# Sparse attention on one Trainium2 core: local keys ahead of selected keys

## The chip, the cores and the metric

The program runs on one core of one Trainium2 chip. The metric is the device time of one execution in microseconds (us); the time before is the median of three runs. One execution was also recorded by the hardware profiler; all rows below are from that one.

A core has five engines that run side by side, each with its own in-order queue: TensorE (PE in the rows; its weight loads are a row of their own, PEld), VectorE (DVE), ScalarE (ACT), GpSimd (POOL) and SyncE (SP), which here issues transfers. They wait for each other by semaphores.

## What is computed

One decoder layer on 512 tokens of width 1024. The part that the change touches is the sparse attention (NSA): 8 query heads in two groups of four (`kv`), each query attending three times, to compressed keys (31 blocks), to selected key blocks and to a local window of 256 keys, with a linear distance bias. The three results are summed with gates:

```
s = einsum(q, k_cmp) - slope * dist;  p_cmp = masked_softmax(s);  o_cmp = p_cmp @ v_cmp
s = einsum(q, kg)    - slope * dist;  p_slc = masked_softmax(s);  o_slc = p_slc @ vg
s = einsum(q, kwb)   - slope * dist;  p_win = masked_softmax(s);  o_win = p_win @ vwb
return gb[..., 0:1] * o_cmp + gb[..., 1:2] * o_slc + gb[..., 2:3] * o_win
```

With 512 tokens all 8 key blocks are selected, so the selected keys are simply all earlier keys. Around this part stand the input projections, gated linear attention (GLA), cross-attention to a memory and a gated convolutional feed-forward layer.

## The kernel before

Matmuls keep fp32 accuracy by splitting each operand into a high and a low part; `split` (lines 164 to 166) makes the high part on ScalarE and the low part, source minus high, on VectorE. A dense product takes three matmuls per tile (lines 160 to 162).

The attention runs over eight blocks, `kv` 0 and 1 with `i` 0 to 3 each; block `i` holds 128 queries. The main loop (lines 695 to 701) writes, for each block, first `nsa_values` of the block before, then `nsa_scores` of this one, then some "fillers": dense products of the GLA stage, two, one, two, one, one, two, none and none of them, which give TensorE work while the softmax runs.

`nsa_scores` makes, for each of four heads `g`, the scores of the selected keys (n = 128(i+1) columns) and of the local keys (nw, up to 384 columns), each added to its bias and reduced to a row maximum in one VectorE instruction (lines 603 and 615). Then come the compressed scores on GpSimd and ScalarE with their row sums (line 627), and eight exponentials on ScalarE (line 631), selected and local in turn, each followed by a read of its row sum. Only then one reciprocal and one product with the gates (lines 634 and 635) make the 12 coefficients `cf` per query. All probabilities are scaled by them: selected keys on VectorE for g 0 to 2 (line 639) and on ScalarE for g 3 (641), local keys on ScalarE for g 0 and 2 (643) and on GpSimd for g 1 and 3 (645), compressed keys on GpSimd (646).

`nsa_values` takes the scaled probabilities key tile by key tile: four transposes into a bank `pt` (line 669, two such banks), a split of that bank, and the products with the values (line 663) into one bank `o`. The order of these jobs is selected, local, compressed; the last, compressed one needs one product, the others two. Two small additions and splits make the block's output.

The order of the instructions on an engine is not the order of this text: the framework's scheduler, when the kernel is built, places an instruction whose operands it expects to be ready ahead of earlier ones that are not. In the trace, filler matmuls (lines 160 to 162, and 197 to 199 of GLA) stand between transposes and products. Once built, the order is fixed.

Of the kernel before, what the change touches and what calls it, by code (L numbers as in the profile page):

```python
# [9 lines left out]
F32 = mybir.dt.float32  # L10
# [6 lines left out]
P = 128  # L17
# [41 lines left out]
def layer_kernel(ctx: ExitStack, tc: tile.TileContext, xT, memT, W, small, const, gfin, out, out_t, order):  # L59
# [19 lines left out]
    def s_(dtype=F32):  # L79
        return sb([P, T], dtype, "s", SB)  # L80
# [6 lines left out]
    def bank(tag):  # L87
        uid[0] += 1
        return psum.tile([P, T], F32, name=f"{stage[0]}_ps_{tag}_{uid[0]}", tag=tag, bufs=BANKS[tag])
# [14 lines left out]
    def C(name):  # L104
        a, b = CO[name]
        return cst[:, a:b]
# [460 lines left out]
    def nsa_scores(kv, i):  # L567
        n = P * (i + 1)
        j0 = max(0, i - 2)
        nw = P * (i + 1 - j0)  # L570
        off = (2 - (i - j0)) * P
        qs = slice(i * P, (i + 1) * P)
        mx = sb([P, 12], F32, "mx", 3)
        sums = sb([P, 12], F32, "sums", 3)
        cm = CM[i % 2][:, :, 0:31]

        def compressed():
            ps = bank("sc")
            pv = ps[:, 0:248].rearrange("p (g n) -> p g n", n=62)
            for g in range(4):  # L580
                nc.tensor.matmul(pv[:, g, :], Q2[kv * 4 + g][:, qs], KC[:, kv, :], start=True, stop=True)
            bias = C("cmp")[:, i * 31:(i + 1) * 31].unsqueeze(1).to_broadcast([P, 4, 31])
            nc.vector.tensor_tensor(cm, pv[:, :, 0:31], bias, op=ALU.add)
            nc.vector.tensor_tensor(cm, pv[:, :, 31:62], cm, op=ALU.add)
            nc.vector.tensor_reduce(mx[:, 0:4], cm, axis=AX.X, op=ALU.max)

        first = kv == 0 and i == 0
        if not first:
            compressed()
        ss, sw = [], []  # L590
        for g in range(4):
            q = Q2[kv * 4 + g][:, qs]
            ps = bank("sc")
            if i < 2:

                both = ps[:, 0:2 * n].rearrange("p (b n) -> p b n", b=2)
                nc.tensor.matmul(both, q, KX[kv][0][:, :, :n], start=True, stop=False)
                nc.tensor.matmul(both, q, KX[kv][1][:, :, :n], start=False, stop=True)
            else:
                nc.tensor.matmul(ps[:, :n], q, KS[kv][0][:, :n], start=True, stop=False)  # L600
                nc.tensor.matmul(ps[:, :n], q, KS[kv][1][:, :n], start=False, stop=True)
            s = s_()
            nc.vector.tensor_tensor_reduce(out=s[:, :n], in0=ps[:, :n], in1=C("slc")[:, 384 - P * i:512],
                                           op0=ALU.add, op1=ALU.max, scale=1.0, scalar=-3e38,
                                           accum_out=mx[:, 4 + g:5 + g])
            ss.append(s)
            if i < 2:
                ps = ps[:, n:2 * n]
            else:
                ps = bank("sc")  # L610
                ks = slice(j0 * P, j0 * P + nw)
                nc.tensor.matmul(ps[:, :nw], q, KW[kv][0][:, ks], start=True, stop=False)
                nc.tensor.matmul(ps[:, :nw], q, KW[kv][1][:, ks], start=False, stop=True)
            s = s_()
            nc.vector.tensor_tensor_reduce(out=s[:, :nw], in0=ps[:, :nw], in1=C("win")[:, off:off + nw],
                                           op0=ALU.add, op1=ALU.max, scale=1.0, scalar=-3e38,
                                           accum_out=mx[:, 8 + g:9 + g])
            sw.append(s)
        if first:
            compressed()  # L620
        nm = sb([P, 12], F32, "nm", 3)
        nc.vector.tensor_mul(nm, mx, C("nslope")[:, kv * 12:(kv + 1) * 12])  # L622
        nc.gpsimd.tensor_tensor(cm, cm, C("slope")[:, kv * 4:kv * 4 + 4].unsqueeze(2).to_broadcast([P, 4, 31]),
                                op=ALU.mult)
        nc.gpsimd.tensor_tensor(cm, cm, nm[:, 0:4].unsqueeze(2).to_broadcast([P, 4, 31]), op=ALU.add)
        nc.scalar.activation(cm, cm, AF.Exp)
        nc.vector.tensor_reduce(sums[:, 0:4], cm, axis=AX.X, op=ALU.add)
        for g in range(4):
            sl = 2.0 ** -(kv * 4 + g + 1)
            for s, c, w in ((ss[g], 4 + g, n), (sw[g], 8 + g, nw)):  # L630
                nc.scalar.activation(s[:, :w], s[:, :w], AF.Exp, scale=sl, bias=nm[:, c:c + 1],  # L631
                                     accum_out=sums[:, c:c + 1])
        cf = sb([P, 3, 4], F32, "cf", 3)
        nc.vector.reciprocal(cf.rearrange("p b g -> p (b g)"), sums)
        nc.vector.tensor_mul(cf, cf, gates[i][:, kv * 12:(kv + 1) * 12].rearrange("p (g b) -> p b g", b=3))
        for g in range(4):
            a, b = ss[g][:, :n], sw[g][:, :nw]
            if g < 3:
                nc.vector.tensor_scalar(a, a, cf[:, 1, g:g + 1], None, op0=ALU.mult)
            else:  # L640
                nc.scalar.activation(a, a, AF.Copy, scale=cf[:, 1, g:g + 1])
            if g % 2 == 0:
                nc.scalar.activation(b, b, AF.Copy, scale=cf[:, 2, g:g + 1])
            else:
                nc.gpsimd.tensor_scalar(b, b, cf[:, 2, g:g + 1], None, op0=ALU.mult)
        nc.gpsimd.tensor_tensor(cm, cm, cf[:, 0, :].unsqueeze(2).to_broadcast([P, 4, 31]), op=ALU.mult)
        return kv, i, j0, ss, sw, CM[i % 2]

    def nsa_values(kv, i, j0, ss, sw, cm):
# [1 line left out]
            for a in range(2):  # L651
                ON[kv * 2 + a] = (g_(F32R), g_(F32R))
        qs = slice(i * P, (i + 1) * P)
        jobs = [([ss[g][:, kt * P:(kt + 1) * P] for g in range(4)], V2[kt][:, kv, :]) for kt in range(i + 1)]
        for kt in range(j0, i + 1):
            jobs.append(([sw[g][:, (kt - j0) * P:(kt - j0 + 1) * P] for g in range(4)], V2[kt][:, 2 + kv, :]))
        jobs.append(([cm[:, g] for g in range(4)], VC[:, kv, :]))
        po = bank("o")
        last = len(jobs) - 1

# [5 lines left out]
        for j, (srcs, v) in enumerate(jobs):  # L666
            pt = bank("pt")
            for g in range(4):
                nc.tensor.transpose(pt[:, g * P:(g + 1) * P], srcs[g], C("ident"))  # L669
            if j < last:  # L670
                h, l = sb([P, T], F32R, "pth", 2), sb([P, T], F32R, "ptl", 2)
                split(h, l, pt)
                parts = (h, l)
            else:
                x = PC[i % 2]
                split(x[0:32], x[32:64], pt[0:32])
                parts = (x,)
            if ready is not None:
                product(*ready)
            ready = (j, v) + parts  # L680
# [635 lines left out]
```

## Time and profile before

| | before |
|---|---|
| median of 3 runs | 865.82 us (863.78 to 866.4) |
| the profiled execution | 864.57 us |
| its span, first to last instruction | 862.7 us |
| TensorE's granted clock, mean | 0.998 of full speed |
| the sparse-attention stage in the span | about 72 to 212 us |

The busy times of the page are shares of the span. In a view of stretches each engine has busy time and, in brackets, instructions started. A waits view names the engine and line that waited, what released it, total time, number of waits and the longest one. A wait of PEld is the weight load's; the matmul before it can still be running.

### The profile page before, as it was taken

The page shows a single profiled execution, that of the slowest core. Times are in us where ns is not written, and L with a number is a line of the kernel's source. Part 1 is how long each engine was busy: PE and PEld are TensorE (multiplying, and loading weights), DVE is VectorE, ACT ScalarE, POOL GpSimd, SP SyncE. Part 2 cuts the span into 40 slices and gives each one's busy share as a digit, 9 for nine tenths or more (in the row PEclk, how much of TensorE's full clock was granted, in tenths as well). Part 3 has the DMA queues.
Part 4 walks back from the last instruction along what each step waited for, and adds up shares of the span by engine and source line. Part 5 has one row for each costly group of instructions (what it writes and reads, how often), then busy time and mean ns, then how long its engine had stood idle before and what let it go on. Part 6 is the DMA issues. An engine that isn't in the chain of part 4 may idle for free.

```text
span 862.7 us, 11076 instructions
## 1 busy us (share of the span) xinstructions
PE 847.2 (98%) x4172; PEld 706.4 (82%) x4172; DVE 565.8 (66%) x923; ACT 425.0 (49%) x742; POOL 176.6 (20%) x157
## 2 busy tenths in 40 slices
PE   9999999999999999999999999999999999999997
PEld 6988788777877888898888888888888888888996
DVE  7576898989979677454587759665533465565324
ACT  8466878787444455344455545433311333334311
POOL 2373354412000023203200412111000111112121
PEclk9999999999999999999999999999999999999999
DMA  8332210102221242254331132222222222222302
GB/s 292 115 131 98 74 50 25 49 25 74 74 91 57 74 147 98 97 178 147 123 115 49 65 110 96 98 98 97 98 98 98 97 98 98 97 98 98 123 25 98
DMA packets 26406, 83.58 MB, mean 97 GB/s; under 512 B 3056, under 2 KB 5104, under 8 KB 26352
## 3 DMA queue, kind: packets, MB, share of 16 engines
q1 hardware_dynamic: 26064, 82.58, 27.5%
q8 instruction: 33, 0.54, 0.2%
q10 hardware_dynamic: 288, 0.28, 0.1%
q14 instruction: 21, 0.17, 0.1%
HBM read 80.76 MB, written 2.10 MB: 96 GB/s over the span
## 4 chain that ended last, share of the span: by engine, by line
PE 87%; DVE 5%; ACT 4%; issue 1%; POOL 1%; DMA 0%; DVEq 0%; ACTq 0%; POOLq 0%
PE up_ps_sc L162 4%; PE up_ps_sc L161 4%; PE up_ps_sc L160 4%; PE fill_ps_acc L160 3%; PE fill_ps_acc L161 3%; PE fill_ps_acc L162 3%; PE up_ps_pt L162 3%; PE up_ps_pt L161 3%; PE up_ps_pt L160 3%; PE up_ps_acc L162 3%; PE up_ps_acc L161 3%; PE up_ps_acc L160 3%; PE nsa_ps_o L663 2%; PE nsa_ps_pt L669 2%; PE down_ps_sc L162 2%; PE down_ps_sc L161 2%
## 5 line engine op out<-in xcount | busy, mean ns | idle before, releaser
L1086 POOL TENSOR_TENSOR up_s<-up_s,up_s 128x512 f32<-128x512 f32 x22 | 35.8, 1630 | 259.1 <-ACT up_wh L140 207.0
L141 DVE TENSOR_TENSOR up_wl<-up_raw,up_wh 128x1024 fp32r<-128x1024 f32 x40 | 63.0, 1575 | 15.4 <-ACT up_wh L140 15.3
L140 ACT ACTIVATE up_wh<-up_raw 128x1024 fp32r<-128x1024 f32 x40 | 42.5, 1061 | 60.9 <-PE up_ps_sc L161 31.9
L160 PE MATMUL up_ps_sc<-xo_g,up_wh 128*128 128x512 f32 x124 | 48.3, 390 | 0.0
L162 PE MATMUL up_ps_sc<-xo_g,up_wl 128*128 128x512 f32 x124 | 48.3, 389 | 0.0
L161 PE MATMUL up_ps_sc<-xo_g,up_wh 128*128 128x512 f32 x124 | 48.3, 389 | 0.0
L160 PE MATMUL up_ps_pt<-xo_g,up_wh 128*128 128x512 f32 x104 | 40.5, 389 | 0.0
L162 PE MATMUL up_ps_pt<-xo_g,up_wl 128*128 128x512 f32 x104 | 40.5, 389 | 0.0
L161 PE MATMUL up_ps_pt<-xo_g,up_wh 128*128 128x512 f32 x104 | 40.5, 389 | 0.0
L160 PE MATMUL fill_ps_acc<-in_g,fill_wh 128*128 128x512 f32 x96 | 38.4, 400 | 0.8 <-DVE fill_t L548 0.8
L161 PE MATMUL fill_ps_acc<-in_g,fill_wh 128*128 128x512 f32 x96 | 38.1, 397 | 0.0
L162 PE MATMUL fill_ps_acc<-in_g,fill_wl 128*128 128x512 f32 x96 | 37.9, 395 | 0.0
L631 ACT ACTIVATE nsa_s<-nsa_s,nsa_nm 128x128 f32<-128x128 f32 (+3 forms) x64 | 34.2, 538 | 6.5 <-DVE nsa_nm L622 6.5
L160 PE MATMUL up_ps_acc<-xo_g,up_wh 128*128 128x512 f32 x88 | 34.3, 389 | 0.0
L162 PE MATMUL up_ps_acc<-xo_g,up_wl 128*128 128x512 f32 x88 | 34.3, 389 | 0.0
L161 PE MATMUL up_ps_acc<-xo_g,up_wh 128*128 128x512 f32 x88 | 34.2, 389 | 0.0
L1082 ACT ACTIVATE up_s<-up_s 128x512 f32<-128x512 f32 x22 | 13.8, 632 | 40.4 <-DVE up_s L1080 40.4
L140 ACT ACTIVATE down_wh<-down_raw 128x1024 fp32r<-128x1024 f32 x9 | 9.5, 1061 | 39.4 <-PE down_ps_sc L161 17.5
L165 ACT ACTIVATE nsa_pth<-nsa_ps_pt 128x512 fp32r<-128x512 f32 x38 | 21.9, 593 | 11.0 <-PE nsa_ps_pt L669 10.7
L161 PEld LDWEIGHTS up_ps_sc<-xo_g,up_wh 128*128 128x128 f32 x124 | 23.3, 188 | 4.9
L160 PEld LDWEIGHTS up_ps_sc<-xo_g,up_wh 128*128 128x128 f32 x124 | 23.3, 188 | 4.8
L162 PEld LDWEIGHTS up_ps_sc<-xo_g,up_wl 128*128 128x128 f32 x124 | 23.3, 188 | 4.8
(975 smaller groups left out, 2687.6 us busy)
## 6 DMA issues: line engine op xcount, KB each, us to landing
up_raw<-in_w SPq DMA_DIRECT2D x44, 512.0 KB, 3.2
fill_raw<-in_w SPq DMA_DIRECT2D x20, 512.0 KB, 3.2
down_raw<-in_w SPq DMA_DIRECT2D x18, 512.0 KB, 3.2
proj_raw<-in_w SPq DMA_DIRECT2D x14, 512.0 KB, 3.8
mix_raw<-in_w SPq DMA_DIRECT2D x12, 512.0 KB, 3.2
mkv_raw<-in_w SPq DMA_DIRECT2D x8, 512.0 KB, 3.3
wout_raw<-in_w SPq DMA_DIRECT2D x8, 512.0 KB, 3.4
in_s<-in_xT SPq DMA_DIRECT2D x8, 256.0 KB, 5.4
```

The lines of the kernel that those rows point to most:

```text
L140: nc.scalar.activation(wh[:, c], r[:, c], AF.Copy)
L141: lo.tensor_tensor(wl[:, c], r[:, c], wh[:, c].bitcast(F32), op=ALU.subtract)
L160: nc.tensor.matmul(ps, w[0], x[0], start=first, stop=False)
L161: nc.tensor.matmul(ps, w[0], x[1], start=False, stop=False)
L162: nc.tensor.matmul(ps, w[1], x[0], start=False, stop=last)
L165: nc.scalar.activation(h, src, AF.Copy)
L631: nc.scalar.activation(s[:, :w], s[:, :w], AF.Exp, scale=sl, bias=nm[:, c:c + 1], accum_out=sums[:, c:c + 1])
L663: nc.tensor.matmul(po, v, x, start=j == 0 and x is parts[0], stop=j == last and x is parts[-1])
L669: nc.tensor.transpose(pt[:, g * P:(g + 1) * P], srcs[g], C("ident"))
L1082: nc.scalar.activation(cv, cv, AF.Gelu_apprx_tanh)
L1086: nc.gpsimd.tensor_tensor(gm, gm, cv, op=ALU.mult)
```

## The change

In `nsa_scores` the local scores and their reduction stand ahead of those of the selected keys. The four exponentials of the local keys come first; then coefficients of compressed and local keys are made by a reciprocal and a product of their own, the local and compressed probabilities are scaled, and only then come the four exponentials of the selected keys, their own reciprocal and product, and their scaling. `nsa_values` takes local keys first, then compressed, then selected ones. The engines of each step stay as they were.

```diff
@@ nsa_scores
             if i < 2:
...
+                pw, ps = ps[:, n:2 * n], ps[:, :n]
             else:
-                nc.tensor.matmul(ps[:, :n], q, KS[kv][0][:, :n], start=True, stop=False)
-                nc.tensor.matmul(ps[:, :n], q, KS[kv][1][:, :n], start=False, stop=True)
+                pw = ps[:, :nw]
+                ks = slice(j0 * P, j0 * P + nw)
+                nc.tensor.matmul(pw, q, KW[kv][0][:, ks], start=True, stop=False)
+                nc.tensor.matmul(pw, q, KW[kv][1][:, ks], start=False, stop=True)
+                ps = bank("sc")[:, :n]
+                nc.tensor.matmul(ps, q, KS[kv][0][:, :n], start=True, stop=False)
+                nc.tensor.matmul(ps, q, KS[kv][1][:, :n], start=False, stop=True)
...
+        def exps(xs, b, w):
+            for g in range(4):
+                c = b * 4 + g
+                nc.scalar.activation(xs[g][:, :w], xs[g][:, :w], AF.Exp, scale=2.0 ** -(kv * 4 + g + 1),
+                                     bias=nm[:, c:c + 1], accum_out=sums[:, c:c + 1])
+
+        def coefficients(b):
+            nc.vector.reciprocal(cf[:, b], s3[:, b])
+            nc.vector.tensor_mul(cf[:, b], cf[:, b], gt[:, b])
+
+
+        exps(sw, 2, nw)
+        coefficients(slice(0, 3, 2))
         for g in range(4):
-            sl = 2.0 ** -(kv * 4 + g + 1)
-            for s, c, w in ((ss[g], 4 + g, n), (sw[g], 8 + g, nw)):
-                nc.scalar.activation(s[:, :w], s[:, :w], AF.Exp, scale=sl, bias=nm[:, c:c + 1],
-                                     accum_out=sums[:, c:c + 1])
-        cf = sb([P, 3, 4], F32, "cf", 3)
-        nc.vector.reciprocal(cf.rearrange("p b g -> p (b g)"), sums)
-        nc.vector.tensor_mul(cf, cf, gates[i][:, kv * 12:(kv + 1) * 12].rearrange("p (g b) -> p b g", b=3))
-        for g in range(4):
-            a, b = ss[g][:, :n], sw[g][:, :nw]
-            if g < 3:
-                nc.vector.tensor_scalar(a, a, cf[:, 1, g:g + 1], None, op0=ALU.mult)
-            else:
-                nc.scalar.activation(a, a, AF.Copy, scale=cf[:, 1, g:g + 1])
+            b = sw[g][:, :nw]
             if g % 2 == 0:
                 nc.scalar.activation(b, b, AF.Copy, scale=cf[:, 2, g:g + 1])
             else:
                 nc.gpsimd.tensor_scalar(b, b, cf[:, 2, g:g + 1], None, op0=ALU.mult)
         nc.gpsimd.tensor_tensor(cm, cm, cf[:, 0, :].unsqueeze(2).to_broadcast([P, 4, 31]), op=ALU.mult)
+        exps(ss, 1, n)
+        coefficients(slice(1, 2))
+        for g in range(4):
+            a = ss[g][:, :n]
+            if g < 3:
+                nc.vector.tensor_scalar(a, a, cf[:, 1, g:g + 1], None, op0=ALU.mult)
+            else:
+                nc.scalar.activation(a, a, AF.Copy, scale=cf[:, 1, g:g + 1])
@@ nsa_values
-        jobs = [([ss[g][:, kt * P:(kt + 1) * P] for g in range(4)], V2[kt][:, kv, :]) for kt in range(i + 1)]
-        for kt in range(j0, i + 1):
-            jobs.append(([sw[g][:, (kt - j0) * P:(kt - j0 + 1) * P] for g in range(4)], V2[kt][:, 2 + kv, :]))
+        jobs = [([sw[g][:, (kt - j0) * P:(kt - j0 + 1) * P] for g in range(4)], V2[kt][:, 2 + kv, :])
+                for kt in range(j0, i + 1)]
+        comp = len(jobs)
         jobs.append(([cm[:, g] for g in range(4)], VC[:, kv, :]))
+        for kt in range(i + 1):
+            jobs.append(([ss[g][:, kt * P:(kt + 1) * P] for g in range(4)], V2[kt][:, kv, :]))
...
-            if j < last:
+            if j != comp:
```

## Rows read from the trace of the kernel before

**Rows 1.** The page: busy time, share of the span and instructions of each engine

```profile
PE 847.2 (98%) x4172; PEld 706.4 (82%) x4172; DVE 565.8 (66%) x923; ACT 425.0 (49%) x742; POOL 176.6 (20%) x157
```

**Rows 2.** Three stretches: length, busy time of each engine (instructions), clock, transfers

```profile
core 0: us, PE busy (x) PEld busy (x) DVE busy (x) ACT busy (x) POOL busy (x), PEclk, DMA share, GB/s
97.00:212.00 115.00, 111.99 (x583) 88.85 (x582) 103.33 (x284) 93.95 (x235) 42.13 (x48) 1.00 0.14 48
240.00:275.00 35.00, 32.66 (x171) 26.71 (x170) 29.65 (x45) 17.17 (x25) 1.05 (x2) 1.00 0.15 51
500.00:800.00 300.00, 300.00 (x1334) 249.54 (x1333) 172.45 (x184) 109.24 (x132) 36.39 (x23) 1.00 0.29 100
```

**Rows 3.** Waits, 72 to 212 us: who, for whom, us in total, times, longest

```profile
POOL nsa_s L645 <- DVE nsa_cf L635: 18.4, 3, 8.4
...
ACT nsa_pth L165 <- PE nsa_ps_pt L669: 10.7, 12, 2.6
...
PEld nsa_ps_o L663 <- DVE nsa_ptl L166: 3.9, 8, 1.1
PEld nsa_ps_pt L669 <- DVE nsa_s L639: 3.3, 9, 0.5
...
PE nsa_ps_o L663 <- DVE nsa_ptl L166: 1.1, 2, 0.6
...
PE nsa_ps_pt L669 <- DVE nsa_s L639: 0.4, 2, 0.2
```

**Rows 4.** TensorE in order of time: start, length, instruction (transposes, and what follows)

```profile
168.35 1.59 PE L669 MATMUL nsa_ps_pt<-in_cst,nsa_s 128*128 128x128 f32 x8
169.70 0.42 PE L613 MATMUL nsa_ps_sc<-in_pair,proj_g 128*128 128x384 f32 x1
...
172.14 0.60 PE L669 MATMUL nsa_ps_pt<-in_cst,nsa_s 128*128 128x128 f32 x4
172.49 0.48 PE L663 MATMUL nsa_ps_o<-nsa_pth,proj_g 128*128 128x512 f32 x1
...
182.61 0.99 PE L669 MATMUL nsa_ps_pt<-in_cst,nsa_s 128*128 128x128 f32 x4
...
184.24 0.47 PE L198 MATMUL gla_ps_sc<-fill_wl,in_g 128*128 128x512 f32 x1
```

**Rows 5.** Lines 631, 634, 635: count, ns least/median/most, first and last start

```profile
L631 ACT ACTIVATE nsa_s<-nsa_s,nsa_nm x64: 385/547/725, 79.9 to 194.0; 128x384 f32<-128x384 f32 x24, 128x128 f32<-128x128 f32 x16, 128x256 f32<-128x256 f32 x16, 128x512 f32<-128x512 f32 x8
L631 ACT ACTIVATION_READ_ACCUMULATOR nsa_s<-nsa_s,nsa_nm x64: 184/187/207, 80.2 to 194.5; 128x1 f32 x64
L634 DVE RECIPROCAL nsa_cf<-nsa_sums x8: 219/228/228, 83.6 to 194.8; 128x12 f32<-128x12 f32 x8
L635 DVE TENSOR_TENSOR nsa_cf<-nsa_cf,proj_gate x8: 155/170/172, 83.9 to 195.1; 128x12 f32<-128x12 f32 x8
```

**Rows 6.** Block kv 1, i 3 in order of time, engine by engine

```profile
190.24 0.19 ACT L631 ACTIVATION_READ_ACCUMULATOR nsa_s<-nsa_s,nsa_nm 128x1 f32 x1
...
196.27 1.11 ACT L643 ACTIVATE nsa_s<-nsa_s,nsa_cf 128x384 f32<-128x384 f32 x2
...
189.89 0.27 DVE L627 TENSOR_REDUCE nsa_sums<-proj_cm 128x4 f32<-128x124 f32 x1
...
194.81 0.23 DVE L634 RECIPROCAL nsa_cf<-nsa_sums 128x12 f32<-128x12 f32 x1
...
195.28 1.88 DVE L639 TENSOR_SCALAR nsa_s<-nsa_s,nsa_cf 128x512 f32<-128x512 f32 x3
...
196.26 0.72 PE L669 MATMUL nsa_ps_pt<-in_cst,nsa_s 128*128 128x128 f32 x4
```

**Rows 7.** GpSimd's scalings of local keys, line 645: blocks of i 0, 1, 3

```profile
84.27 1.19 POOL L645 TENSOR_SCALAR nsa_s<-nsa_s,nsa_cf 128x128 f32<-128x128 f32 x2 [3.23 <-ACT fill_t L549]
104.12 1.84 POOL L645 TENSOR_SCALAR nsa_s<-nsa_s,nsa_cf 128x256 f32<-128x256 f32 x2 [6.89 <-DVE nsa_cf L635]
...
195.41 2.84 POOL L645 TENSOR_SCALAR nsa_s<-nsa_s,nsa_cf 128x384 f32<-128x384 f32 x2 [8.42 <-DVE nsa_cf L635]
```

More of the change, by code (lines that the diff above doesn't have):

```diff
@@ L598, in nsa_scores @@
                 nc.tensor.matmul(both, q, KX[kv][1][:, :, :n], start=False, stop=True)
+                pw, ps = ps[:, n:2 * n], ps[:, :n]
             else:
-                nc.tensor.matmul(ps[:, :n], q, KS[kv][0][:, :n], start=True, stop=False)
-                nc.tensor.matmul(ps[:, :n], q, KS[kv][1][:, :n], start=False, stop=True)
-            s = s_()
-            nc.vector.tensor_tensor_reduce(out=s[:, :n], in0=ps[:, :n], in1=C("slc")[:, 384 - P * i:512],
+                pw = ps[:, :nw]
[5 more added lines that the diff above has]
+                nc.tensor.matmul(ps, q, KS[kv][1][:, :n], start=False, stop=True)
+            s = s_()
+            nc.vector.tensor_tensor_reduce(out=s[:, :nw], in0=pw, in1=C("win")[:, off:off + nw],
+                                           op0=ALU.add, op1=ALU.max, scale=1.0, scalar=-3e38,
+                                           accum_out=mx[:, 8 + g:9 + g])
+            sw.append(s)
+            s = s_()
+            nc.vector.tensor_tensor_reduce(out=s[:, :n], in0=ps, in1=C("slc")[:, 384 - P * i:512],
                                            op0=ALU.add, op1=ALU.max, scale=1.0, scalar=-3e38,
@@ L606, in nsa_scores @@
             ss.append(s)
-            if i < 2:
-                ps = ps[:, n:2 * n]
-            else:
[L610 to L618, printed above, removed]
         if first:
@@ L627, in nsa_scores @@
         nc.vector.tensor_reduce(sums[:, 0:4], cm, axis=AX.X, op=ALU.add)
-        for g in range(4):
-            sl = 2.0 ** -(kv * 4 + g + 1)
-            for s, c, w in ((ss[g], 4 + g, n), (sw[g], 8 + g, nw)):
-                nc.scalar.activation(s[:, :w], s[:, :w], AF.Exp, scale=sl, bias=nm[:, c:c + 1],
-                                     accum_out=sums[:, c:c + 1])
-        cf = sb([P, 3, 4], F32, "cf", 3)
-        nc.vector.reciprocal(cf.rearrange("p b g -> p (b g)"), sums)
-        nc.vector.tensor_mul(cf, cf, gates[i][:, kv * 12:(kv + 1) * 12].rearrange("p (g b) -> p b g", b=3))
-        for g in range(4):
-            a, b = ss[g][:, :n], sw[g][:, :nw]
-            if g < 3:
-                nc.vector.tensor_scalar(a, a, cf[:, 1, g:g + 1], None, op0=ALU.mult)
-            else:
-                nc.scalar.activation(a, a, AF.Copy, scale=cf[:, 1, g:g + 1])
+        cf = sb([P, 3, 4], F32, "cf", 3)
+        gt = gates[i][:, kv * 12:(kv + 1) * 12].rearrange("p (g b) -> p b g", b=3)
+        s3 = sums.rearrange("p (b g) -> p b g", g=4)
+        def exps(xs, b, w):
[8 more added lines that the diff above has]
+        coefficients(slice(0, 3, 2))
+        for g in range(4):
+            b = sw[g][:, :nw]
             if g % 2 == 0:
```

## The prediction

> **What bounds the kernel now.** I read the page's busy times first, then the same by stretches, then the waits of the stretch that the change touches, and at last the order of time around three blocks. TensorE is busy 98% of the span and no other engine over 66% [rows 1], so time can only leave through gaps and slow spots on TensorE. From 500 to 800 us there are none: 300.00 of 300 us. In the sparse-attention stretch, 97 to 212 us, TensorE is busy 111.99 of 115 us, and VectorE 103.33, or 90% [rows 2]. TensorE bounds that stretch too, with VectorE right behind it, and ScalarE at 93.95.
>
> The 3.0 us that TensorE is not busy there are not all that can be won, because a matmul that waits for its stationary operand looks longer and not idle. The weight-load row sees more: in the stage it stood idle or late 3.3 us in 9 waits on the scaled scores of the selected keys (line 639), and the matmul row 0.4 us in 2 for the same cause; the products of line 663 waited 3.9 and 1.1 us for the low parts that VectorE makes (line 166) [rows 3]. The order of time shows it: eight transposes take 168.35 to 169.70, 1.35 us, where four elsewhere take 172.14 to 172.49, 0.35 us, so 0.65 us are lost; 182.61 to 184.24 holds eight in 1.63 us, 0.9 us lost [rows 4]. So two sums frame the stake: 3.7 us for transposes that come before their coefficients are applied, and 5.0 us for products that come before their split is done.
>
> Beside the matmul row one may weigh the weight loads. They are busy 88.85 of 115 us here (77%) against 249.54 of 300 (83%) in the dense stretch [rows 2]. The Trainium skill (Perfetto Trace Analysis, Identifying the Most-Contended Engine) says that the matmul row flatters TensorE and that weight-load time is the better gauge; by it the room would be an estimated (0.83 - 0.77) x 115 = 7 us, near the sum of the two waits, and not the 3.0 us of the matmul row.
>
> **The change part by part.** TensorE's work is the same: the same scores, 46 groups of four transposes and the same products, in another order. So are the 64 exponentials and their 64 sum reads, at 0.547 and 0.187 us in the middle [rows 5].
>
> *A. The first transposes of a block wait for four exponentials, not eight.* Today coefficients are made once, after all eight. Block kv 1, i 3 shows it [rows 6]: the fourth sum is read at 190.24, four more follow, the reciprocal (line 634) starts at 194.81, three scalings run on VectorE from 195.28 for 1.88 us, and the first transposes start at 196.26 and are drawn out to 0.72 us. With local keys first, their coefficients can be made at about 190.6, once the fourth sum is read. The scaled local columns come last from GpSimd, whose two scalings took 2.84 us here [rows 7]: about 0.4 + 2.84 us later, so near 193.8. That is 2.4 us before 196.26. The selected keys come later than now, by the two ScalarE copies that step ahead of their exponentials, 1.11 us [rows 6]; but three groups of local keys and one of compressed keys stand in front of them. Each such group needs one split on VectorE, so the wait that line 639 ends today is mostly covered by these. Bounds: nothing to 3.7 us. I take two thirds, 2.5 us, since blocks with one local key tile have little in front of the selected keys.
>
> *B. ScalarE and VectorE work more evenly.* ScalarE stood idle 10.7 us in 12 waits for transposes before its splits [rows 3], most of it just after the scalings. With local transposes available during the selected keys' exponentials this hole is filled, the splits run earlier, and some of the 5.0 us on line 166 goes. But the split's own latency stays in front of every product, and the order on each engine is fixed before the run: fills stand among the products in a pattern that the scheduler chose from its own estimates, so what is late next is again a product behind its split. Bounds: 0 to 5.0 us. I take 1.0 us.
>
> *C. One more reciprocal and one more product on VectorE in each of 8 blocks.* The pair costs 0.228 + 0.170 us for 12 columns [rows 5]. I take the same for 8 and for 4 columns, as these are small already, so 8 x 0.4 = 3.2 us more on an engine that is 90% busy. Its cover is TensorE's fill. TensorE passes on VectorE's delay only where it waits for it: the 3.7 and 5.0 us of waits are 8.7 of 115 us, 8% [rows 2, 3], so 0.3 us at the least; without cover all 3.2 us. I take 0.6 us, nearer the lower end.
>
> *D. The local columns' scalings move onto the path.* They stay on ScalarE (g 0, 2) and GpSimd (g 1, 3). Before, the selected keys' jobs hid them. GpSimd needs 1.19 us for two at i 0, 1.84 at i 1, and 2.84 at i 3, which I take for i 2 as well; ScalarE 1.11 us for two at the largest size [rows 6, 7]. If TensorE comes to these transposes no earlier than GpSimd is done, nothing is lost; that is my value, since today GpSimd was idle in its queue 18.4 us waiting for these very coefficients [rows 3] and now gets them about 4 us earlier. The other end is a rival below. The compressed columns are scaled on GpSimd behind them, and wait for nothing else.
>
> The Trainium skill (GPSIMD Engine Reference, Engine selection) calls one-input work on GpSimd roughly line-rate, and gives 1.03 cycles per element at 1.2 GHz where the body is bound by its ports (section 3.1), by which two times 384 columns would take an estimated 0.7 us and D could cost nothing at all. The row has 2.84 us for two, four times that; the row decides, and so the rival below keeps its price.
>
> *E. Edits with one answer.* For i of 2 or 3 the local scores take their bank first; banks and matmuls are as many. For i below 2 only VectorE's reading order changes. No DMA moves, so SP's queue issues as before. The last group of a block is now one of the selected keys with two products, where it was the compressed one with a single product: one 128x512 matmul of about 0.23 us (the pitch of a dense stretch, 300 us over 1334 matmuls, [rows 2]), once, at the last block's end: 0.2 us at most, beside the next stage's matmuls.
>
> New waits: the first reciprocal waits for the fourth local sum and for the compressed sums (line 627); behind it on VectorE stand the score reductions of the next block and splits, for which TensorE's products wait. The two ScalarE copies wait for it, with the selected keys' exponentials behind them where the scheduler leaves them there.
>
> **Sum.** -2.5 - 1.0 + 0.6 + 0 + 0.2 = -2.7 us. Part of it, I think, comes back later: 240 to 275 us has TensorE busy 32.66 of 35 us [rows 2] in a chain of its own on VectorE (29.65 us), and an earlier end of the stage brings that chain forward with less dense work to lie beside it. I give back 0.6 us: -2.1 us. The profiled execution has a span of 862.7 us and a time of 864.57, 1.9 us around it; so 860.6 us of span and 862.5 us. It lies 1.25 us under the median of the runs, 865.82, so the forecast for the median is 865.82 - 2.1 = 863.7 us.
>
> **The rivals.**
> 1. *Both waits go* (faster). If the even load lets nearly all of A and half to all of B go, with C at its least: 3.7 + 2.5 - 0.3 = 5.9 at the middle, 8.4 at most, less what is given back: about 861.0 us. For it: ScalarE's 10.7 us of holes, and GpSimd's 18.4. Against: the split's latency is not touched.
> 2. *GpSimd ends the wait* (slower). The order is fixed beforehand, so if the local transposes are placed where ScalarE's copies are done, TensorE stands before the columns of g 1 and g 3 until GpSimd is done: 2.84 - 1.11 = 1.7 us in four blocks, and, with copies of 128 and 256 columns put at half of GpSimd's time, 0.9 in two and 0.6 in two: 9.9 us in all. The gain A is then gone. With half of it not covered: +4.9 + 0.6 - 1.0 = +4.5, 870.3 us. It decides as soon as over 3.7 us of these 9.9 reach TensorE. For it: two scalings on GpSimd take longer than three on VectorE (2.84 against 1.88 us). Against: no row of the waits names GpSimd as what TensorE waited for in this stage [rows 3].
> 3. *The split of the coefficients does not come early.* The reciprocal for local and compressed keys needs line 627, which ran at 189.89, just before the fourth sum at 190.24 [rows 6]. Where GpSimd or VectorE makes it later, local coefficients come with the selected ones, and only C is left: +0.6, 866.4 us. Against: in this block it was in time.
>
> **How the numbers follow.** A measurement of this kernel can tell about 0.3%, 2.6 us, from no change: faster is below 863.2, slower above 868.4. Forecast case 0.40, around 863.7 with an own range of 862.2 to 865.2; rival 1 0.22, around 861.0; rival 2 0.20, around 870.3 and from 867 on; rival 3 0.18, around 866.4. Faster: all of rival 1 and nearly half of the forecast case, 0.40. Slower: most of rival 2 and a little of rival 3, 0.21. Same: 0.39. The range leaves out 0.1 at each side: the lower half of rival 1 below 859.5, the upper half of rival 2 above 870.
>
> **What would show it.** A: the reciprocal appears 16 times, the first of each pair some 3 to 4 us ahead of the second; the waits of transposes on line 639's successor fall under 1.5 us. B: ScalarE's idle time before splits falls from 10.7 us to under 6. C: VectorE's busy time rises by about 3 us. D: no TensorE wait on GpSimd; if there are some with over 3 us in all, rival 2 holds. If the gaps only move to the stretch from 212 to 300 us, the giving back was sized too small.

## The result, and the profile after

| | before | after |
|---|---|---|
| median of 4 runs each | 865.07 us (863.78 to 866.40) | 871.20 us (870.17 to 871.38) |
| profiled execution, span | 862.7 us | 869.6 us (871.38 us in all) |

The change costs 6.1 us: ratio 1.0067, 95% interval 1.0051 to 1.0083. The forecast was 2.1 us of gain, with a range of 859.5 to 870.0 us. Executions of one kernel fall into groups by their mean granted clock, 0.998 or 0.996 some 1.5 us above it and a few at 0.992 another 3 us up, so differences below are also given between executions of equal clock; by that measure the change costs 5 to 6 us.

Rows of a view that an argument does not need are left out of the blocks below.

The page's busy times, after; they answer to [rows 1]:

```profile
PE 849.9 (98%) x4172; PEld 706.7 (81%) x4172; DVE 566.3 (65%) x939; ACT 424.4 (49%) x742; POOL 181.8 (21%) x157
```

The same work on TensorE, 4172 instructions, and nearly the same sums on the others. The page alone doesn't show where 6 us went. The stretches do (length, then busy time and instructions of PE, PEld, DVE, ACT and POOL, then the granted clock):

```profile
97.00:135.00 38.00, 34.99 (x173) 26.90 (x173) 34.37 (x101) 27.39 (x68) 15.41 (x15) 1.00 0.12 42
135.00:182.00 47.00, 43.12 (x229) 34.42 (x229) 43.57 (x132) 37.12 (x104) 18.21 (x22) 1.00 0.13 46
182.00:212.00 30.00, 29.00 (x152) 22.52 (x151) 27.09 (x62) 25.66 (x59) 8.11 (x10) 1.00 0.12 44
```

From 97 to 212 us TensorE is busy 34.99 + 43.12 + 29.00 = 107.11 us, against 111.99 in [rows 2], and over the stretch as one it starts 551 matmuls instead of 583. So 4.9 of the 6.9 us between the two profiled spans are lost inside the very stage; most of the rest is a fall of the granted clock at 279 us, about 1.6 us, shown at the end. VectorE's 105.03 us stand against 103.33, though the added coefficient work has its place here.

The waits of 72 to 212 us (who, for whom, us in total, times, longest), in answer to [rows 3]:

```profile
ACT nsa_pth L165 <- PE nsa_ps_pt L683: 9.7, 9, 2.8
PEld nsa_ps_o L677 <- DVE nsa_ptl L166: 7.1, 14, 1.5
PEld nsa_ps_o L677 <- ACT nsa_pth L165: 3.4, 7, 1.7
PE nsa_ps_o L677 <- DVE nsa_ptl L166: 2.7, 3, 1.1
PEld nsa_ps_pt L683 <- POOL nsa_s L649: 2.6, 5, 0.8
PE nsa_ps_o L677 <- DVE proj_pc L166: 2.0, 2, 1.4
PEld nsa_ps_o L677 <- DVE proj_pc L166: 1.6, 4, 1.1
PE nsa_ps_pt L683 <- POOL nsa_s L649: 1.3, 3, 0.6
```

Line 683 holds the transposes (669 before), 677 the products (663), 649 GpSimd's scalings (645), 656 VectorE's scalings of the selected keys (639). Three things are to be seen. No transpose waits for line 656 any more, where 3.7 us waited for line 639: that wait is gone. In its place transposes wait 2.6 + 1.3 = 3.9 us for GpSimd. And products wait 7.1 + 2.7 = 9.8 us for VectorE's low parts, where they waited 5.0, and 3.6 us for those of the compressed keys. Their waits for ScalarE's high parts (line 165) rose too, on the weight loads from 0.5 to 3.4 us.

One block, kv 0, i 3, in order of time (start, length, engine and line), shows both new waits at once:

```profile
136.97 0.20 DVE L638 RECIPROCAL nsa_cf<-nsa_sums 128x8 f32<-128x8 f32 x1 [0.91 <-ACT nsa_s L634]
137.55 2.48 POOL L649 TENSOR_SCALAR nsa_s<-nsa_s,nsa_cf 128x384 f32<-128x384 f32 x2 [3.22 <-ACT nsa_pth L165]
140.08 0.55 PE L683 MATMUL nsa_ps_pt<-in_cst,nsa_s 128*128 128x128 f32 x3 [0.50 <-POOL nsa_s L649]
142.43 0.17 DVE L638 RECIPROCAL nsa_cf<-nsa_sums 128x4 f32<-128x4 f32 x1
142.87 1.29 POOL L540 TENSOR_TENSOR fill_g<-fill_t,fill_t 128x512 f32<-128x512 f32 x1 [1.14 <-DVE nsa_cf L639]
142.90 1.54 DVE L656 TENSOR_SCALAR nsa_s<-nsa_s,nsa_cf 128x512 f32<-128x512 f32 x1
144.37 2.05 DVE L656 TENSOR_SCALAR nsa_s<-nsa_s,nsa_cf 128x512 f32<-128x512 f32 x2
144.66 1.47 POOL L539 TENSOR_TENSOR fill_g<-fill_t,fill_g 128x512 f32<-128x512 f32 x1
147.07 0.50 PE L677 MATMUL nsa_ps_o<-nsa_ptl,proj_g 128*128 128x512 f32 x1 [0.96 <-DVE nsa_ptl L166]
```

The first coefficients come 5.5 us ahead of the second. GpSimd then scales for 2.48 us, and TensorE stands 0.50 us before the transposes of its columns. Having done its scalings early, GpSimd turns to its filler products (lines 539 and 540, two tensors in, one out) just when VectorE scales the selected keys: three scalings take 142.90 to 146.42, 3.5 us, where before three of the same size took 1.88 us [rows 6] beside GpSimd's own scalings [rows 7]. The splits queued behind them on VectorE come late, and a product waits 0.96 us.

### The profile page after: what moved, and what is told of

Its sections match the earlier page's. It is cut to its first block, busy times and chain, and to the rows that moved or that the text cites. A ratio compares the mean times of both kernels' runs of the same rounds, so it can differ in the third digit from the quotient of the medians.

```text
span 869.6 us, 11118 instructions
## 1 busy us (share of the span) xinstructions
PE 849.9 (98%) x4172; PEld 706.7 (81%) x4172; DVE 566.3 (65%) x939; ACT 424.4 (49%) x742; POOL 181.8 (21%) x157
## 4 chain that ended last, share of the span: by engine, by line
PE 85%; ACT 6%; DVE 6%; issue 1%; POOL 1%; DVEq 0%; POOLq 0%; ACTq 0%
PE up_ps_sc L162 4%; PE up_ps_sc L161 4%; PE up_ps_sc L160 4%; PE fill_ps_acc L160 3%; PE fill_ps_acc L162 3%; PE up_ps_pt L162 3%; PE up_ps_pt L161 3%; PE up_ps_pt L160 3%; PE fill_ps_acc L161 3%; PE up_ps_acc L162 3%; PE up_ps_acc L161 3%; PE up_ps_acc L160 2%; PE down_ps_sc L162 2%; PE down_ps_sc L161 2%; PE down_ps_sc L160 2%; ACT nsa_s L634 2%
## 5 line engine op out<-in xcount | busy, mean ns | idle before, releaser
L1100 POOL TENSOR_TENSOR up_s<-up_s,up_s 128x512 f32<-128x512 f32 x22 | 40.2, 1828 | 254.7 <-ACT up_wh L140 202.9
L141 DVE TENSOR_TENSOR up_wl<-up_raw,up_wh 128x1024 fp32r<-128x1024 f32 x40 | 59.3, 1484 | 15.5 <-ACT up_wh L140 15.3
L634 ACT ACTIVATE nsa_s<-nsa_s,nsa_nm 128x384 f32<-128x384 f32 (+3 forms) x64 | 34.2, 537 | 5.2 <-DVE nsa_nm L621 5.1
L166 DVE TENSOR_TENSOR nsa_ptl<-nsa_ps_pt,nsa_pth 128x512 fp32r<-128x512 f32 x38 | 25.4, 684 | 3.1 <-ACT nsa_pth L165 2.6
```

Source lines behind the costliest of these rows:

```text
L141: lo.tensor_tensor(wl[:, c], r[:, c], wh[:, c].bitcast(F32), op=ALU.subtract)
L166: nc.vector.tensor_sub(l, src, h.bitcast(F32))
L634: nc.scalar.activation(xs[g][:, :w], xs[g][:, :w], AF.Exp, scale=2.0 ** -(kv * 4 + g + 1), bias=nm[:, c:c + 1], accum_out=sums[:, c:c + 1])
L1100: nc.gpsimd.tensor_tensor(gm, gm, cv, op=ALU.mult)
```

## The experiments

The two suspects were GpSimd's scaling, now on the path ("GpSimd theory" in the expectations), and VectorE slowed beside GpSimd's products ("port theory"). Their rival, the "reshuffle theory", says that any new order costs as much, because the fillers suit only the old one. The last column is the difference to the kernel before, run beside it, between medians of executions at clock 0.998; e1 and e5 had none at that clock:

| run | what it is | median us | ratio [95%] | at equal clock |
|---|---|---|---|---|
| e1 | new job order alone | 875.05 | 1.0111 [1.0084, 1.0138] | - |
| e6 | e1, engines exchanged | 865.46 | 1.0012 [0.9990, 1.0034] | 0.0 |
| e5 | the change, engines exchanged | 871.01 | 1.0063 [1.0038, 1.0087] | - |
| e2 | the change, old job order | 866.60 | 1.0021 [1.0006, 1.0036] | +2.0 |
| e7 | e2, one-input products | 863.77 | 0.9989 [0.9970, 1.0008] | -0.8 |
| e3 | the change, one-input products | 866.59 | 1.0017 [1.0004, 1.0030] | +1.6 |
| e4 | before, one-input products | 863.31 | 0.9981 [0.9966, 0.9997] | -1.1 |
| e9 | the change, no scaling on GpSimd | 868.60 | 1.0027 [1.0010, 1.0044] | +2.5 |
| e10 | e9, one-input products | 863.90 | 0.9977 [0.9961, 0.9993] | -0.6 |
| e11 | before, no scaling on GpSimd | 867.48 | 1.0041 [1.0018, 1.0065] | +3.0 |
| e8 | scores and maxima first alone | 867.14 | 1.0026 [1.0011, 1.0042] | +2.6 |
| e12 | e8, one-input products | 865.19 | 0.9999 [0.9982, 1.0016] | +0.6 |

### The job order and GpSimd: e1, e6, e5

e1 puts the new order of jobs, and the new place of the single product, into the kernel before.

```
-        jobs = [([ss[g][:, kt * P:(kt + 1) * P] for g in range(4)], V2[kt][:, kv, :]) for kt in range(i + 1)]
-        for kt in range(j0, i + 1):
-            jobs.append(([sw[g][:, (kt - j0) * P:(kt - j0 + 1) * P] for g in range(4)], V2[kt][:, 2 + kv, :]))
+        jobs = [([sw[g][:, (kt - j0) * P:(kt - j0 + 1) * P] for g in range(4)], V2[kt][:, 2 + kv, :])
+                for kt in range(j0, i + 1)]
+        comp = len(jobs)
         jobs.append(([cm[:, g] for g in range(4)], VC[:, kv, :]))
+        for kt in range(i + 1):
+            jobs.append(([ss[g][:, kt * P:(kt + 1) * P] for g in range(4)], V2[kt][:, kv, :]))
...
-            if j < last:
+            if j != comp:
```

> The kernel before with one part of the change: the jobs of nsa_values in the new order (local, compressed, selected); scores, exponentials and coefficients as before. GpSimd theory (TensorE now comes to the local transposes before GpSimd has scaled g 1 and g 3): the wait is here in full, since the two GpSimd scalings still start with the coefficients; 2 to 4 us slower than the kernel before, with TensorE and weight-load waits on GpSimd of 3 us or more. Port theory (VectorE's scalings of the selected keys now run beside GpSimd's two-input fillers and take two to three times as long, and products behind the next split wait): those scalings still run beside GpSimd's one-input scalings, as before, so little of the loss is here, 0 to 1.5 us. Reshuffle theory (fill counts suit only the old order, any new order costs the same): 3 to 6 us slower.

It cost 10.7 us (875.05 against 864.39), the most of all runs and more than any of the three theories expected. Its waits of 72 to 220 us:

```profile
PEld nsa_ps_pt L671 <- POOL nsa_s L645: 9.7, 9, 2.2
PE nsa_ps_pt L671 <- POOL nsa_s L645: 7.7, 7, 2.0
```

17.4 us of transposes behind GpSimd: two scalings of 384 columns cannot be hidden if the local keys go first and their coefficients come last. Part of the loss is the clock, which fell twice behind such waits in this execution (granted clock 0.71 over 172 to 176 us, 0.73 over 192 to 196). e6 keeps that job order and gives the local columns to VectorE and ScalarE, the selected ones to ScalarE and GpSimd:

```
             if g < 3:
-                nc.vector.tensor_scalar(a, a, cf[:, 1, g:g + 1], None, op0=ALU.mult)
+                nc.vector.tensor_scalar(b, b, cf[:, 2, g:g + 1], None, op0=ALU.mult)
...
             if g % 2 == 0:
-                nc.scalar.activation(b, b, AF.Copy, scale=cf[:, 2, g:g + 1])
+                nc.scalar.activation(a, a, AF.Copy, scale=cf[:, 1, g:g + 1])
             else:
-                nc.gpsimd.tensor_scalar(b, b, cf[:, 2, g:g + 1], None, op0=ALU.mult)
+                nc.gpsimd.tensor_scalar(a, a, cf[:, 1, g:g + 1], None, op0=ALU.mult)
```

> The job order alone (which was 10.5 us slower than the kernel before) with the engines of the scalings exchanged as in e5. GpSimd theory: the 17.4 us of waits on GpSimd go, and most of the 10.5 us with them; between 1 us faster and 3 us slower than the kernel before. Reshuffle theory: still 7 us slower or more.

10.7 us of loss became 0.9 (none at equal clock): for the job order alone the cause is GpSimd, and the reshuffle theory, 7 us or more, is out there. e5 makes the same exchange in the changed kernel.

> The changed kernel with the engines of the scalings exchanged: local columns on VectorE (g 0 to 2) and ScalarE (g 3), selected columns on ScalarE (g 0, 2) and GpSimd (g 1, 3). The order of the change stays. Theory so far: two causes, the local transposes that wait for GpSimd (3.9 us of waits in the changed kernel) and VectorE's scalings of the selected keys beside GpSimd's two-input fillers. Both are gone here: VectorE's scalings come when GpSimd has little to do, GpSimd's come last in the job order. Expected 2 to 6 us faster than the changed kernel, that is from 1 us faster than the kernel before to 3 us slower; no wait of TensorE on GpSimd over 0.5 us in the local transposes. Rival (reshuffle): 4 to 8 us slower than the kernel before, as the changed one.

No gain: missed. The order of time shows what took the place of the wait on GpSimd:

```profile
141.39 3.10 POOL L658 TENSOR_SCALAR nsa_s<-nsa_s,nsa_cf 128x512 f32<-128x512 f32 x2
144.46 1.26 POOL L539 TENSOR_TENSOR fill_g<-fill_t,fill_g 128x512 f32<-128x512 f32 x1
145.68 0.39 POOL L624 TENSOR_TENSOR proj_cm<-proj_cm,nsa_nm 128x124 f32<-128x124 f32 x1
146.11 0.31 ACT L625 ACTIVATE proj_cm<-proj_cm 128x124 f32<-128x124 f32 x1 [3.39 <-POOL proj_cm L624]
148.10 0.50 PE L677 MATMUL nsa_ps_o<-nsa_pth,proj_g 128*128 128x512 f32 x1 [2.98 <-ACT nsa_pth L165]
148.00:152.00 4.00, 3.90 (x17) 3.21 (x18) 3.79 (x12) 4.00 (x15) 0.43 (x1) 0.70 0.00 0
```

The selected columns are wider, 3.10 us for two, and GpSimd's small step for the next block's compressed keys (line 624) is queued behind them and a product. ScalarE waits 3.39 us for it, with a high part queued behind that wait, and TensorE waits 2.98 us for the high part. GpSimd still held TensorE, by way of ScalarE. Behind that wait the granted clock fell: 0.70 over 148 to 152 us, the last row. So e5 doesn't speak against GpSimd; it moved the load to another place in the same queue.

### VectorE beside GpSimd's products: e4, e3, e2, e7

These kernels leave one factor out of GpSimd's filler products, so that each reads one tensor. They run longer (1.49 to 2.08 us in e3, where the products took 1.28 to 1.90 in the changed kernel). The factor left out also no longer has to be ready, so the edit loosens a wait besides:

```
-            nc.gpsimd.tensor_tensor(q, q, e1, op=ALU.mult)
+            nc.gpsimd.tensor_scalar(q, q, 1.0, None, op0=ALU.mult)
...
-            nc.gpsimd.tensor_tensor(k1, kf, k1, op=ALU.mult)
-            nc.gpsimd.tensor_tensor(k2, kf, e3, op=ALU.mult)
+            nc.gpsimd.tensor_scalar(k1, k1, 1.0, None, op0=ALU.mult)
+            nc.gpsimd.tensor_scalar(k2, e3, 1.0, None, op0=ALU.mult)
...
-            nc.gpsimd.tensor_tensor(s, th, rf, op=ALU.mult)
+            nc.gpsimd.tensor_scalar(s, th, 1.0, None, op0=ALU.mult)
```

> The kernel before with GpSimd's two-input products of the fillers (gla_q, gla_k, gla_r) replaced by one-input scalings of the same size; it leaves out the second factor of these products. All theories: within 1.5 us of the kernel before, as only one scaling (0.93 us) and one copy (1.02 us) ran beside such a product there.

> The changed kernel with GpSimd's two-input products of the fillers (gla_q, gla_k, gla_r) replaced by one-input scalings of the same size on the same engine; it leaves out the second factor of these products. To be read against its pair, the kernel before with the same replacement. Port theory: VectorE's longest scaling of the selected keys falls from 1.54 us to under 0.9 us, the three long product waits (1.1, 1.0 and 1.4 us) mostly go, and the distance to its pair is 3 us or less, where it was 6. GpSimd theory and reshuffle theory: the distance to its pair stays 5 to 7 us.

The kernel before gains 1.1 us by it, the changed one 4.3 (870.17 to 865.88 at clock 0.998; 4.0 at 0.996), and the distance of the pair is 2.7 us, as the port theory expected. The three scalings of kv 0, i 3, which took 3.5 us in the changed kernel, take 2.02 in e3, beside GpSimd's one-input scaling, and the longest of all took 0.875 us where it was 1.54:

```profile
142.07 2.02 DVE L656 TENSOR_SCALAR nsa_s<-nsa_s,nsa_cf 128x512 f32<-128x512 f32 x3
```

So about 3 us of the loss need GpSimd's second input. The waits on GpSimd stay in e3 at 2.7 + 1.3 us, as they were. e2 is the change with the job order of before, e7 the same with one-input products.

> The changed kernel with the jobs of nsa_values back in the old order (selected, local, compressed); local scores, exponentials and coefficients stay first. GpSimd theory: the local columns are ready long before they are asked for, so no wait on GpSimd; between 1 us faster and 2 us slower than the kernel before. Port theory: VectorE's scalings of the selected keys run behind GpSimd's own, beside its fillers, so single ones take 1.4 us and more; 2 to 5 us slower, as the selected transposes come first and wait for them. Reshuffle theory: 3 to 6 us slower.

> The coefficients and scores of the change with the old job order (2.2 us slower than the kernel before), and GpSimd's two-input products of the fillers replaced by one-input scalings; it leaves out the second factor of these products. To be read against the kernel before with the same replacement, which was 1.1 us faster than the kernel before. Port theory: the 9.7 us of waits on VectorE's scalings of the selected keys fall to under 5 us and the distance to that pair is between 1.5 us faster and 1 us slower. Reshuffle theory: still 2 us slower than that pair, or more.

e2 has no transpose waiting on GpSimd, and loses 2 us; its transposes wait 5.8 + 3.9 us on VectorE's scaling of the selected keys, more than before the change, as that scaling falls beside the products. e7 takes this off: these waits are 3.1 + 1.0 us, and it stands 0.4 us (equal clock) to 0.5 us (medians) above e4. Early coefficients cost next to nothing then, but they bring no gain either.

### Both at once: e9, e10, e11

e9 takes the local scalings from GpSimd without giving it others:

```
-            if g % 2 == 0:
+            if g != 1:
                 nc.scalar.activation(b, b, AF.Copy, scale=cf[:, 2, g:g + 1])
             else:
-                nc.gpsimd.tensor_scalar(b, b, cf[:, 2, g:g + 1], None, op0=ALU.mult)
+                nc.vector.tensor_scalar(b, b, cf[:, 2, g:g + 1], None, op0=ALU.mult)
```

> The changed kernel with GpSimd taken out of the scalings of the local columns: rows g1 go to VectorE, rows g3 to ScalarE, the selected columns stay as they are. Nothing of GpSimd's then stands between the coefficients and TensorE, and its queue (products of the maxima of the next block) gets shorter, not longer as in e5. Theory (GpSimd's own scaling ends the wait for the local columns, about 4 us of TensorE waits on it in the changed kernel, the rest of the loss is VectorE slowed beside GpSimd's two-input products and a fall of the clock): waits of the transposes on GpSimd 0, ratio to the kernel before about 1.002 to 1.004, 866.5 to 868.5 us. Rival (the loss is in the order of the work, whoever scales): no change to the changed kernel, 870.5 to 871.5 us. Second rival (VectorE, 90% busy in this stage, is now later with the selected columns): waits on them rise and the time is above 871.5 us.

868.6 us, a little above the range expected, since most of its executions were at the lower clock; at equal clock it is 866.8, 3.4 us under the changed kernel, and no transpose waits on GpSimd. e10 is e9 with one-input products.

> e9 with GpSimd's products of the gated-attention factors reading one input, as in e3 and e4 (q, k1, k2 and s keep only one of their two factors, so the outputs that rest on them are not the reference's). Both suspected causes are gone at once. Theory: they are all of the loss, so the time is that of the kernel before with one-input products (863.3 us in e4) within 0.7 us, 862.6 to 864.0 us. Rival (a third cause, such as the clock's fall at 279 us or the wait of the compressed product in the middle, holds a part of its own): 864.5 to 866.6 us, the last being e3's time.

863.9 us, within 0.6 us of e4: with both causes off, the changed kernel is as long as the kernel before with one-input products. (e4 still has GpSimd's local scalings; a kernel before with neither was not run.) It isn't shorter, though its transposes wait less. The waits of 72 to 212 us say why, first e4, then e10:

```profile
PEld nsa_ps_o L663 <- DVE nsa_ptl L166: 3.1, 8, 0.9
PEld nsa_ps_pt L669 <- DVE nsa_s L639: 2.9, 7, 0.8
PE nsa_ps_pt L669 <- DVE nsa_s L639: 1.2, 5, 0.4
PEld nsa_ps_o L663 <- ACT nsa_pth L165: 0.5, 2, 0.3
PE nsa_ps_o L663 <- DVE nsa_ptl L166: 0.5, 1, 0.5
```

```profile
PEld nsa_ps_o L677 <- ACT nsa_pth L165: 4.7, 11, 0.9
PEld nsa_ps_o L677 <- DVE nsa_ptl L166: 2.5, 9, 0.5
PEld nsa_ps_o L677 <- DVE proj_pc L166: 1.4, 2, 1.0
PE nsa_ps_o L677 <- ACT nsa_pth L165: 1.1, 3, 0.5
PEld nsa_ps_pt L683 <- ACT nsa_s L647: 1.1, 3, 0.6
PE nsa_ps_o L677 <- DVE proj_pc L166: 1.0, 2, 0.6
```

The 4.1 us on VectorE's scaling are gone, and the products wait 5.8 us instead of 0.5 for ScalarE's high parts; all waits of products on splits in these rows rise from 4.1 to 10.7 us. ScalarE now has splits between exponentials, in a fixed order, and in e9 and e10 also one more scaling per block. Which of the two makes its high parts late is not shown: in e3, without that scaling, products wait only 2.1 us for them, but 6.9 for VectorE's low parts and 2.0 for those of the compressed keys, 11.0 in all.

e11 makes e9's exchange in the kernel before, where the local columns are wanted last.

> The kernel before with the same exchange as e9: local columns of rows g1 on VectorE, g3 on ScalarE, none on GpSimd. There the local columns are wanted last, so GpSimd's scaling ends no wait. Theory: no gain, and a small loss if GpSimd's two-input products now fall beside VectorE's scalings (they came after its scalings before): 864.0 to 867.0 us. Rival (GpSimd's scalings cost the kernel before as well): 861.5 to 863.5 us, which would be faster than both kernels.

It lost 3.0 us at equal clock, and its median is just above the range expected. Without its scalings, GpSimd reaches its filler products earlier, while VectorE scales:

```profile
123.79 1.27 POOL L552 TENSOR_TENSOR fill_g<-fill_t,fill_t 128x512 f32<-128x512 f32 x1
123.84 1.43 DVE L639 TENSOR_SCALAR nsa_s<-nsa_s,nsa_cf 128x384 f32<-128x384 f32 x1
125.67 0.41 DVE L639 TENSOR_SCALAR nsa_s<-nsa_s,nsa_cf 128x384 f32<-128x384 f32 x1
```

A scaling of 384 columns beside the product takes 1.43 us, the next, past it, 0.41. Transposes wait 7.3 + 3.3 us for line 639, where it was 3.7. So in the kernel before GpSimd's slow scalings did a second service: they kept its products off VectorE's way. VectorE and ScalarE also have one more scaling per block in e11; what that costs was not parted from it.

### The order of the scores: e8, e12

e8 takes from the change only that scores and maxima of the local keys come first.

```
-            nc.vector.tensor_tensor_reduce(out=s[:, :n], in0=ps[:, :n], in1=C("slc")[:, 384 - P * i:512],
+            nc.vector.tensor_tensor_reduce(out=s[:, :nw], in0=pw, in1=C("win")[:, off:off + nw],
...
```

> The kernel before with local scores and their maxima ahead of those of the selected keys, and nothing else of the change. Both main theories: nothing that TensorE waits for moves, within 1 us of the kernel before. Reshuffle theory: 2 us slower or more.

It lost 2.6 us with no work added, as the reshuffle theory alone expected. One row pair of it looked like the same contention, a product of 128 x 12 numbers at 1.15 us, which took 0.170 in [rows 5]:

```profile
166.97 1.30 POOL L540 TENSOR_TENSOR fill_g<-fill_t,fill_t 128x512 f32<-128x512 f32 x1 [1.28 <-ACT fill_t L536]
167.14 1.15 DVE L634 TENSOR_TENSOR nsa_cf<-nsa_cf,proj_gate 128x12 f32<-128x12 f32 x1
```

> e8 (only the scores and maxima of the local keys first) with GpSimd's products of the gated-attention factors reading one input, as in e3, e4 and e7 (q, k1, k2 and s keep only one of their two factors, so the outputs that rest on them are not the reference's). e8 took 867.1 us, 2.5 us more than the kernel before, although no work is added. Theory (the new order only shifts GpSimd's two-input products beside VectorE's work on SBUF; in e8 the small product of the coefficients took 1.15 us instead of 0.17 beside such a product): the loss is gone, within 0.7 us of the kernel before with one-input products (863.3 us), 862.6 to 864.0 us. Rival (the order of the scores costs by itself, by the banks they wait for): still some 2 us above that, 865.0 to 866.2 us.

e12's median lies in the rival's range, 865.0 to 866.2 us; at equal clock it is 864.8, 0.6 us over the kernel before and 1.6 us over e4. The second input explains 1.0 of e8's 2.6 us. The rest is a cost of this order when coefficients come late; e7 has the same score order with early coefficients and stands within 0.4 us of e4. In the waits the rest shows on products: 5.9 us for low parts and 2.0 for high parts in e12, 3.6 and 0.5 in e4. Why the splits come later there wasn't settled. The parts of the change don't add up.

## Why the prediction was wrong

**What bounds the kernel** was read rightly: the loss shows as waits and late matmuls of TensorE, 4.9 of 6.9 us inside the stage, with VectorE right behind it.

**A (-2.5 us): the mechanism held, the gain did not arrive.** Coefficients came early (5.5 us in the block shown) and the 3.7 us of transposes behind line 639 went to none. The step that failed is what is late next. The prediction named products behind their split, but counted the wait removed as won. In the changed kernel the products' waits on splits rose from 5.7 to 17.0 us. e10, with both suspects off, shows the exchange: against e4, 4.1 us of transpose waits removed, 6.6 us more of product waits, no time won.

**B (-1.0 us): wrong sign.** ScalarE's idle time before splits fell from 10.7 to 9.7 us only, where under 6 was to be seen, and the waits on line 166 rose from 5.0 to 9.8 us, and to 5.5 + 1.4 us even without the contention (e3).

**C (+0.6 us): right count, wrong price.** The 16 pairs, after (count, then ns least/median/most):

```profile
L638 DVE RECIPROCAL nsa_cf<-nsa_sums x16: 165/184/203, 81.9 to 200.2; 128x8 f32<-128x8 f32 x8, 128x4 f32<-128x4 f32 x8
L639 DVE TENSOR_TENSOR nsa_cf<-nsa_cf,proj_gate x16: 150/163/1248, 82.2 to 200.4; 128x8 f32<-128x8 f32 x8, 128x4 f32<-128x4 f32 x8
```

Medians of 0.184 and 0.163 us agree with the 0.4 us taken for a pair. VectorE's busy time from 97 to 212 us rose 1.7 us, where about 3 was to be seen. The longest product, 1.248 us for 128 x 4 numbers at 173.11, is the point that was missed. Every duration of the kernel before was carried over as if it belonged to the instruction. It belongs to the instruction and to what GpSimd does beside it: moving GpSimd's 2.84 us of scalings forward moved its fillers' products onto VectorE's scalings. This term stood nowhere in the sum, and cost about 3 us (4.0 to 4.3 in the changed kernel by e3, less 1.1 in the kernel before by e4). One such case stood in the trace of the kernel before, a scaling of 256 columns beside line 540's product (166.81 to 168.15), where 0.34 us is usual:

```profile
167.37 0.93 DVE L639 TENSOR_SCALAR nsa_s<-nsa_s,nsa_cf 128x256 f32<-128x256 f32 x1
```

**D (0): failed.** "If TensorE comes to these transposes no earlier than GpSimd is done, nothing is lost" was the condition, and TensorE came earlier: 3.9 us of waits, and 2.1 us of time by e3 and e10 (865.88 to 863.78), 3.4 us by e9. GpSimd's 18.4 us of idle time said that it was free when the coefficients came; it did not say that its 2.5 us fit into the lead.

Rival 2 had this place, a point of 3.7 us from which it decides, and 870.3 us; 3.9 us and 871.2 were measured. But its price came out near by chance: GpSimd's scaling alone accounts for 2 to 3.4 us, and most of the rest is the contention, which no rival held. **E** put the new order of the scores at nothing. By itself (e8) it cost 2.6 us, 1.6 without the contention (e12); beside early coefficients, again without it, about 0.4 (e7). Its share in the whole change can't be read apart. Rival 3 shows in one block at the most: in kv 0, i 1 the two reciprocals lie 0.5 us apart. The 0.6 us given back plays no part, since nothing was won.

The terms as measured, at clock 0.998: contention 3.2 us (4.3 less 1.1), GpSimd on the path 2.1, rest 0.6 (e10 over e4), together the 5.9 us between the one execution of the changed kernel at that clock, 870.17, and 864.3. They add up by construction, as each is taken from the one before. Taken the other way round, by e9 first, GpSimd on the path is 3.4 us and contention 1.9 (3.0 from e9 to e10, less 1.1): the two overlap. No version beat both kernels with the whole computation in it; e6 came equal to the kernel before.

## What to carry to other kernels

When an engine's work is moved forward, ask what it does in the time that comes free: here GpSimd's next two-input products fell on VectorE's scalings, which no view of busy time of the kernel before shows. Before moving a job to the head of a chain, compare the slowest engine's time for it, not the mean, with the lead that the move gives. And a wait that is removed is a gain only once the next operand's producer, here the splits on ScalarE and VectorE, is shown to be early too.

## What the runs showed of the hardware

**VectorE is held beside GpSimd's two-input products.** A scaling of 128x512 took 1.54 us beside such a product of 1.29 us (the block above), where in the same execution one with no product beside it took 0.48:

```profile
201.40 0.48 DVE L656 TENSOR_SCALAR nsa_s<-nsa_s,nsa_cf 128x512 f32<-128x512 f32 x1
```

One of 128x384 took 1.43 us beside a product, one beside none 0.41 (e11). Beside GpSimd's one-input scalings, three of 128x512 took 1.88 us together [rows 6, 7], against 3 x 0.48 alone. GpSimd is held in its turn. One of its products took 1.90 us where most take 1.29; it started while VectorE made the low part of a weight, source minus high part. VectorE's small product of coefficients, 0.16 us in most blocks, took 1.25 beside it:

```profile
171.90 1.29 DVE L141 TENSOR_TENSOR gla_wl<-fill_raw,gla_wh 128x1024 fp32r<-128x1024 f32 x1
172.44 1.90 POOL L540 TENSOR_TENSOR fill_g<-fill_t,fill_t 128x512 f32<-128x512 f32 x1 [0.33 <-ACT fill_t L536]
173.11 1.25 DVE L639 TENSOR_TENSOR nsa_cf<-nsa_cf,proj_gate 128x4 f32<-128x4 f32 x1
```

The Trainium skill (SBUF — State Buffer, SBUF: two separate sides) calls the pair of ports that the two engines share an exclusive lock: whichever instruction starts first has it to its end. Beside the two-input products the rows agree, as a scaling ends only some 0.2 to 0.3 us after the product does (144.44 against 144.16 in the block above, 125.27 against 125.06 in e11), and in the last three rows GpSimd's product ends 1.15 us after the split, the coefficients right behind it. For VectorE's scalings beside one-input scalings they don't: 1.88 us for three could not be if each waited for a scaling of 1.4 us to end. Yet a one-input scaling of GpSimd's that started beside such a split, at 92.76, took 2.32 us where 1.50 is usual.

**A clock fall behind a wait.** In the profiled execution of the changed kernel (start, length; then a stretch with its busy times and granted clock):

```profile
278.52 0.50 PE L160 MATMUL fill_ps_acc<-nsa_g,fill_wh 128*128 128x512 f32 x1 [1.50 <-DVE fill_g L731]
279.66 0.63 PE L161 MATMUL fill_ps_acc<-nsa_g,fill_wh 128*128 128x512 f32 x1
280.09 0.63 PE L162 MATMUL fill_ps_acc<-nsa_g,fill_wl 128*128 128x512 f32 x1
282.97 0.39 PE L160 MATMUL fill_ps_acc<-nsa_g,fill_wh 128*128 128x512 f32 x1
```

```profile
279.00:283.00 4.00, 4.00 (x13) 3.09 (x12) 2.98 (x4) 1.99 (x4) 0.00 (x0) 0.57 0.47 162
```

After 1.50 us of waiting, starts lie 0.43 us apart where 0.23 is usual: the granted clock is at the lower of its two levels (1.2 of 2.4 GHz) from about 279.5 to 282.8, which costs about 1.6 us. The kernel before has the same wait of 1.50 us at 273.38 in its profiled execution, with no fall behind it:

```profile
273.38 0.50 PE L160 MATMUL fill_ps_acc<-nsa_g,fill_wh 128*128 128x512 f32 x1 [1.50 <-DVE fill_g L717]
273.73 0.40 PE L161 MATMUL fill_ps_acc<-nsa_g,fill_wh 128*128 128x512 f32 x1
```

The profiled executions of e8, e9 and e12, mean clock 0.996 or 0.997, show a fall between 260 and 300 us as well, those of e3, e4 and e10 none from 72 to 440 us. What decides between the two was not tried.
